# A decoder layer on one core: three waits in the first projection, the bias table and the last accumulators, and 256 columns of the last norm given to other engines

## The chip, the cores and the metric

The kernel runs on one core of a Trainium2 chip. A core has a matmul engine (TensorE, "PE" in the profile; its weight loads are listed apart as "PEld"), VectorE ("DVE"), ScalarE ("ACT"), GpSimd ("POOL") and SyncE ("SP", which only issues DMAs here). Each engine works through its own list of instructions in the order in which the program wrote it, and waits on semaphores for the others. The metric is the device time of one launch in microseconds (us).

## The reference

One decoder layer for x of 256 tokens by 2048 features, all in float32:

```
proj = x @ w_in                      # 2048 -> 18,768 columns: queries, shared latent, gates, indexer, RG-LRU input
attn = sparse attention: indexer scores, the best 64 keys of each query, softmax with a T5
       relative-position bias rel_bias[bucket(distance)], values projected up per head
h    = RG-LRU: causal depthwise convolution of width 4, gates, scan over the tokens
merged = sigmoid(g_A) * ((attn * silu(gate_a)) @ w_branch_a)
       + sigmoid(g_B) * ((h * silu(gate_b)) @ w_branch_b)
out  = layernorm(2**0.25 * x + merged @ w_out) * ln_g + ln_b
```

The three places of this change are the first part of the projection, the table of the relative-position bias, and the end: the product with w_out and the layer norm.

## The kernel before, in words

**Split operands.** Every float32 matrix is taken apart into a high part and a low part: `hi_of` (L97, ScalarE) copies it rounded to the type that TensorE takes, and `lo_of` (L101, VectorE) subtracts that copy from the original. A product is then the sum of three: high by high, high by low and low by high. So each weight tile costs a load (SP), a `hi` (ScalarE) and a `lo` (VectorE) before TensorE can use it.

**The first projection (L219 to L275).** The loop over k (16 steps of 128 features) multiplies all tokens by 848 columns (latent, indexer weights and key: psc; the first four query tiles of the indexer: psq). In step k the program writes, in this order: `split_a(k + 1)` for the next step, the loads, TensorE's products of step k, and from k = 12 on one call of `split_to`, which splits the first halves of the weight tiles of the main loop (`raw`, four buffers; `hi` and `lo`, five buffers each). All that stands on ScalarE and VectorE in the order in which it is written.

**The main loop.** The other columns and products are jobs, each of 4 or 16 ticks. In every tick TensorE gets its products, then `tick(t)` lets every helper whose time has come write its next step (a helper is a generator; `yield n` makes it sleep n ticks), and every second tick `split_to` and `load_to` write the split of the half that is five ahead and the load of the one that is nine ahead. TensorE uses one half in two ticks of a column job.

**The table.** `rel` (L424) is such a helper, started at tick 25. It issues the load of the one-hot buckets, writes the high part of the 32 x 16 bias values, sleeps, writes their low part on VectorE (L429), sleeps, and writes the two matmuls psrel (L434). ScalarE copies their result and GpSimd's DMAs lay it out for the attention heads.

**The end.** The product with w_out is made in four column groups of 512. For the first three (pso) both token blocks (t = 0 and 1, 128 tokens each) run together; `residual` adds alpha * x on VectorE (L828) and takes the statistics of the result with bn_stats (L829). For t = 0 it writes its result into `y` (SBUF), for t = 1 back into the accumulator (PSUM). The fourth group (psz) is made for t = 0 whole, and then for t = 1 in two halves of 256 columns; `normalise` for t = 0 is written between the two. `acc_tile` hands out four accumulator banks in turn.

`normalise` (L840) joins the statistics (L844), starts the square root (ScalarE L291, VectorE L292 to L299), and then treats the columns in pieces of 512. Three of four go through VectorE: `centre` (L851: subtract the mean, multiply by ln_g) and `finish` (L854: multiply by the root, add ln_b), followed by a store issued from SP (L855). The piece from column 1024 goes another way: ScalarE subtracts the mean (L860), GpSimd multiplies by ln_g (L861), ScalarE multiplies by the root (L868), GpSimd adds ln_b (L869), and ScalarE issues the store (L870).

Of the kernel before, what the change touches and what calls it, by code (L numbers as in the profile page):

```python
# [13 lines left out]
AF = mybir.ActivationFunctionType  # L14
# [4 lines left out]
P = 128  # L19
# [54 lines left out]
def layer(ctx, tc, ar, out):  # L74
    nc = tc.nc
# [20 lines left out]
    def hi_of(hi, src):  # L96
        nc.scalar.activation(hi, src, AF.Copy)  # L97

    def lo_of(lo, src, hi):

        nc.vector.tensor_sub(lo, src, f(hi))  # L101

    def acc_tile(name):
        return psum.tile([P, 512], F32, name=name, tag="acc", bufs=4)
# [4 lines left out]
    def slot(name, dt=F32R):  # L109
        return big.tile([P, 2 * T], dt, name=name, tag="slot", bufs=16)  # L110
# [68 lines left out]
    def split_to(n):  # L179
        while st["split"] < min(n, len(halves)):  # L180
            i = st["split"]
            load_to(i + 1)
            raw = raws.pop(i)
            if NO + 24 <= i < NO + 28:
                pieces = []
                for e in range(2):
                    hi, lo = slot(f"wh{i}_{e}"), slot(f"wl{i}_{e}")
                    c = raw[:, e * 512:(e + 1) * 512]
                    hi_of(hi, c)
                    lo_of(lo, c, hi)  # L190
                    pieces.append((hi, lo))
                parts[i] = pieces
            else:
                hi = wpool.tile([P, 1024], F32R, name=f"hi{i}", tag="hi", bufs=5)
                lo = wpool.tile([P, 1024], F32R, name=f"lo{i}", tag="lo", bufs=5)
                hi_of(hi, raw)
                lo_of(lo, raw, hi)
                parts[i] = (hi, lo)
            st["split"] += 1
# [21 lines left out]
    with pool("pha", side="right") as pha:  # L221
        ins = {}

        def load_a(k):
            xr = pha.tile([P, T], F32, name=f"xr{k}", tag="xr", bufs=4)
            nc.sync.dma_start(xr, ar["xT"][k])
            wr = pha.tile([P, NA], F32, name=f"wr{k}", tag="wr", bufs=4)
            if k == 0:
                nc.scalar.dma_start(wr[:, :A_Q], ar["wA"][k][:, :A_Q])
                nc.sync.dma_start(wr[:, A_Q:], ar["wA"][k][:, A_Q:])  # L230
            else:
                nc.sync.dma_start(wr, ar["wA"][k])
            ins[k] = (xr, wr)

        def split_a(k):
            xr, wr = ins.pop(k)
            hi_of(xs[:, k, :T], xr)
            lo_of(xs[:, k, T:], xr, xs[:, k, :T])
            hi = pha.tile([P, NA], F32R, name=f"ahi{k}", tag="ahi", bufs=3)
            lo = pha.tile([P, NA], F32R, name=f"alo{k}", tag="alo", bufs=3)  # L240
            for c in ([slice(0, A_Q), slice(A_Q, NA)] if k < 3 else [slice(0, NA)]):
                hi_of(hi[:, c], wr[:, c])
                lo_of(lo[:, c], wr[:, c], hi[:, c])
            return hi, lo

        for k in range(4):
            load_a(k)
        smalls = [(params, ar["params"]), (causal, ar["causal"]), (kvg, ar["kvg"].to_broadcast([P, DL])),
                  (relb, ar["relb"])]
        sp = {0: split_a(0)}  # L250
        for k in range(KT):
            if k + 1 < KT:
                sp[k + 1] = split_a(k + 1)
            if k + 4 < KT:
                load_a(k + 4)
            else:
                load_to(st["load"] + 1)
            if 8 <= k < 12:
                nc.sync.dma_start(*smalls[k - 8])
            hi, lo = sp.pop(k)  # L260
            fl = (k == 0, k == KT - 1)
            for t in range(2):
                o = psc[t][:, :A_Q]
                x_hi = xs[:, k, t * P:(t + 1) * P]
                x_lo = xs[:, k, T + t * P:T + (t + 1) * P]
                nc.tensor.matmul(o, x_hi, hi[:, :A_Q], start=fl[0], stop=False)
                nc.tensor.matmul(o, x_hi, lo[:, :A_Q], start=False, stop=False)
                nc.tensor.matmul(o, x_lo, hi[:, :A_Q], start=False, stop=fl[1])
            last = k == KT - 1
            for high in (False, True) if last else (True, False):  # L270
                for i in range(4):
                    w = (hi if high else lo)[:, A_Q + i * P:A_Q + (i + 1) * P]
                    mm(psq[i], w, xs[:, k, :], high, fl[0] and high, last and high)
            if k >= 12:
                split_to(k - 11)  # L275

    def evac(ps, name, dst=None):

# [145 lines left out]
    def rel():  # L424
        oh = idx.tile([32, VL], F32R, name="oh")
        nc.gpsimd.dma_start(oh, ar["onehot"])
        rb = idx.tile([32, 2, NH], F32R, name="rb")
        hi_of(rb[:, 0, :], relb)
        yield 6  # L429
        lo_of(rb[:, 1, :], relb, rb[:, 0, :])  # L430
        yield 2
        ps = aux_tile("psrel")
        for e in range(2):
            nc.tensor.matmul(ps[:NH, :], rb[:, e, :], oh, start=e == 0, stop=e == 1)  # L434
        yield
        v = idx.tile([NH, VL], F32, name="vrel")
        nc.scalar.activation(v, ps[:NH, :], AF.Copy, scale=DL ** 0.5)
        yield
        nc.gpsimd.dma_start(dv, v)
        for g in range(NH // HG):  # L440
            nc.gpsimd.dma_start(dz[g], bass.AP(tensor=dv.tensor, offset=dv.offset + g * SLAB,
                                               ap=[[0, P], [1, SLAB]]).rearrange("p (h v) -> p h v", h=HG))
            yield 10

    bias = {}
# [333 lines left out]
    for kind, i in jobs:  # L779
        rhs = us if kind in ("ba", "bb") else {k: xs[:, k, :] for k in range(KT)}  # L780
        chunk = kind in CHUNKS
        ps = [acc_tile(f"ps_{kind}{i}_{t}") for t in range(2)] if chunk else acc_tile(f"ps_{kind}{i}")
        for qt in range(ticks((kind, i))):
            t = at[kind, i] + qt
# [8 lines left out]
            if t == G0 + 14:  # L793
                rnn_stack.close()
                dec_stack = ExitStack()
                v = dec_stack.enter_context(pool("dec", side="right")).tile([P, 16, T], F32, name="decay")
            if t == FIN:
                dec_stack.close()
                fin = ctx.enter_context(pool("fin", side="right"))
                y = [fin.tile([P, DM], F32, name=f"y{e}") for e in range(2)]  # L800
                gb = [fin.tile([P, DM], F32, name=f"gb{e}") for e in range(2)]
# [4 lines left out]
            else:  # L806
                high = qt in (0, 3)
                w = parts[t // 2][0 if high else 1]
                for kk in range(8):
                    k = qt // 2 * 8 + kk  # L810
# [12 lines left out]
    tmp = [fin.tile([P, 4], F32, name=f"lt{t}") for t in range(2)]  # L823
# [14 lines left out]
    rows = []  # L838

    def normalise(t, ne):  # L840


        mean = mv[t][:, 0:1]
        nc.vector.bn_aggr(mv[t], st6[t][:, :ne, :])  # L844
        mine = [(c, v) for u, c, v in rows if u == t]
        (rest, v3), = [r for r in mine if r[0].start == 1024]
        mine.remove((rest, v3))
        yr = y[t][:, rest]

        def centre(c, v):  # L850
            nc.vector.scalar_tensor_tensor(v, v, mean, gb[0][:, c], op0=OP.subtract, op1=OP.mult)  # L851

        def finish(c, v):
            nc.vector.scalar_tensor_tensor(y[t][:, c], v, r, gb[1][:, c], op0=OP.mult, op1=OP.add)  # L854
            nc.sync.dma_start(out[t * P:(t + 1) * P, c], y[t][:, c])  # L855

        root = rsqrt(mv[t][:, 1:2], [tmp[t][:, i:i + 1] for i in range(3)], 1.0)
        next(root)
        nc.vector.tensor_scalar(tmp[t][:, 3:4], mean, -1.0, None, op0=OP.mult)
        nc.scalar.activation(yr, v3, AF.Identity, bias=tmp[t][:, 3:4])  # L860
        nc.gpsimd.tensor_mul(yr, yr, gb[0][:, rest])  # L861
        centre(*mine[0])
        next(root)
        try:
            next(root)
        except StopIteration as e:
            r = e.value
        nc.scalar.activation(yr, yr, AF.Identity, scale=r)  # L868
        nc.gpsimd.tensor_add(yr, yr, gb[1][:, rest])  # L869
        nc.scalar.dma_start(out[t * P:(t + 1) * P, rest], yr)  # L870
        finish(*mine[0])
        for m in mine[1:]:
            centre(*m)
            finish(*m)
# [16 lines left out]
    last = range(NO + 24, NO + 32)  # L891
    cuts = [[slice(0, 512)], [slice(0, 256), slice(256, 512)]]
    for t in range(2):
        ps = acc_tile(f"psz{t}")
        for e, c in enumerate(cuts[t]):
            for n in last:
                for i in range(2):
                    d = 2 * (n - NO - 24) + i
                    products(ps[:, c], parts[n], i, d, xs[:, d, :], t, c)
                tick(t0)  # L900
                t0 += 1
                split_to(len(halves))
            residual(t, slice(3 * 512 + c.start, 3 * 512 + c.stop), 3 + e, ps[:, c])
        rows[-len(cuts[t]):] = [(t, slice(3 * 512, 4 * 512), ps if t else y[t][:, 3 * 512:])]
        normalise(t, 3 + len(cuts[t]))
    assert not agenda, agenda

# [51 lines left out]
```

## Time and profile before

| what | us |
|---|---|
| median of 3 runs | 1035.03 (1034.36 to 1035.72) |
| profiled execution | 1034.45 |
| its span, first to last instruction | 1032.7 |
| TensorE busy | 1015.0 (98%) |
| VectorE busy | 678.8 (66%) |
| ScalarE busy | 551.6 (53%) |
| GpSimd busy | 82.0 (8%) |

The profile is one execution. A timeline lists an engine's instructions as start, duration, engine, line, operation, tile written and tiles read, their shapes, and in square brackets how long the engine stood idle before it and what ended that. A chain of waits goes back from the last instruction to whatever released each one. Times are us from the start of the span.

### The profile page before, as it was taken

How to read it: one execution, taken by the hardware profiler on the slowest of the kernel's cores; microseconds unless marked ns; L12 is line 12 of the kernel's file. 1: busy time of each engine (PE TensorE's matmuls, PEld its weight loads, DVE VectorE, ACT ScalarE, POOL GpSimd, SP SyncE). 2: the span in 40 equal slices, each digit the busy share in tenths (PEclk: the TensorE clock that was granted, in tenths of full speed). 3: DMA queues.
4: the chain of work that ended last, by engine and by line, in shares of the span. 5: the costliest groups of instructions: out<-in, count | busy, mean ns of one | idle time of the engine just before them, and what ended most of it. 6: DMA issues, size and time to landing. Idle time of an engine off the chain costs nothing.

```text
span 1032.7 us, 14867 instructions
## 1 busy us (share of the span) xinstructions
PE 1015.0 (98%) x5464; PEld 881.0 (85%) x5464; DVE 678.8 (66%) x1147; ACT 551.6 (53%) x910; POOL 82.0 (8%) x120
## 2 busy tenths in 40 slices
PE   9999999999999999999999999999999999999994
PEld 8888888998999988888888888888888888888884
DVE  6668775677677766544454888855577875566565
ACT  6666654555555565444334566588655554444431
POOL 0004312001111100000000000000500000000002
PEclk9999999999999999999999999999999999999997
DMA  9745877656566565665667666556666678666632
GB/s 306 265 144 171 276 252 233 194 171 178 170 189 174 183 184 162 185 191 196 192 196 213 196 186 194 171 183 190 193 190 185 200 252 283 186 192 190 186 120 82
DMA packets 61000, 201.41 MB, mean 195 GB/s; under 512 B 6608, under 2 KB 13136, under 8 KB 59904
## 3 DMA queue, kind: packets, MB, share of 16 engines
q1 hardware_dynamic: 59264, 191.29, 60.1%
q0 software_dynamic: 1232, 8.49, 2.1%
q8 instruction: 43, 0.70, 0.3%
q10 hardware_dynamic: 432, 0.70, 0.2%
q14 instruction: 29, 0.24, 0.1%
HBM read 198.31 MB, written 6.32 MB: 198 GB/s over the span
## 4 chain that ended last, share of the span: by engine, by line
PE 96%; DVE 2%; DMA 1%; issue 0%; ACT 0%; SPq 0%; DVEq 0%; ACTq 0%
PE ps_q L204 17%; PE ps_ag L204 9%; PE ps_rg L204 9%; PE ps_xr L204 9%; PE ps_ga L776 3%; PE ps_bb L776 3%; PE ps_gb L776 3%; PE ps_gb L775 3%; PE ps_ga L774 3%; PE ps_bb L774 3%; PE ps_ba L776 3%; PE ps_ba L774 3%; PE ps_bb L775 3%; PE ps_ga L775 3%; PE ps_gb L774 3%; PE ps_ba L775 3%
## 5 line engine op out<-in xcount | busy, mean ns | idle before, releaser
L101 DVE TENSOR_TENSOR lo<-raw,hi 128x1024 fp32r<-128x1024 f32 x324 | 399.5, 1234 | 307.1 <-ACT hi L97 303.3
L97 ACT ACTIVATE hi<-raw 128x1024 fp32r<-128x1024 f32 x324 | 341.5, 1054 | 175.6 <-PE ps_ba L776 52.6
L204 PE MATMUL ps_q<-xs,hi 128*128 128x512 f32 x512 | 122.4, 391 | 0.0
L204 PEld LDWEIGHTS ps_q<-xs,hi 128*128 128x128 f32 x512 | 94.0, 188 | 18.3
L204 PE MATMUL ps_q<-xs,lo 128*128 128x256 f32 x512 | 71.2, 283 | 0.0
L204 PEld LDWEIGHTS ps_q<-xs,lo 128*128 128x128 f32 x512 | 66.3, 190 | 1.4
L204 PE MATMUL ps_ag<-xs,hi 128*128 128x512 f32 x256 | 61.2, 391 | 0.0
L204 PE MATMUL ps_rg<-xs,hi 128*128 128x512 f32 x256 | 61.2, 391 | 0.0
L204 PE MATMUL ps_xr<-xs,hi 128*128 128x512 f32 x256 | 61.2, 391 | 0.0
L204 PEld LDWEIGHTS ps_rg<-xs,hi 128*128 128x128 f32 x256 | 47.1, 188 | 9.1
L204 PEld LDWEIGHTS ps_ag<-xs,hi 128*128 128x128 f32 x256 | 47.1, 188 | 9.1
L204 PEld LDWEIGHTS ps_xr<-xs,hi 128*128 128x128 f32 x256 | 47.0, 188 | 9.1
L774 PE MATMUL ps_bb<-hi,ub 128*128 128x512 f32 x128 | 50.4, 393 | 0.0
L774 PE MATMUL ps_ga<-hi,xs 128*128 128x512 f32 x128 | 50.0, 391 | 0.0
L776 PE MATMUL ps_bb<-hi,ub 128*128 128x512 f32 x128 | 49.9, 390 | 0.0
L776 PE MATMUL ps_ga<-hi,xs 128*128 128x512 f32 x128 | 49.9, 390 | 0.0
L776 PE MATMUL ps_gb<-hi,xs 128*128 128x512 f32 x128 | 49.9, 390 | 0.0
L775 PE MATMUL ps_gb<-lo,xs 128*128 128x512 f32 x128 | 49.8, 389 | 0.0
L775 PE MATMUL ps_ga<-lo,xs 128*128 128x512 f32 x128 | 49.8, 389 | 0.0
L775 PE MATMUL ps_bb<-lo,ub 128*128 128x512 f32 x128 | 49.8, 389 | 0.0
L774 PE MATMUL ps_ba<-hi,ua 128*128 128x512 f32 x128 | 49.8, 389 | 0.0
L775 PE MATMUL ps_ba<-lo,ua 128*128 128x512 f32 x128 | 49.8, 389 | 0.0
(273 smaller groups left out, 1888.7 us busy)
## 6 DMA issues: line engine op xcount, KB each, us to landing
raw<-in_wt SPq DMA_DIRECT2D x168, 512.0 KB, 4.2
raw<-in_wga SPq DMA_DIRECT2D x32, 512.0 KB, 3.6
raw<-in_wba SPq DMA_DIRECT2D x32, 512.0 KB, 3.5
raw<-in_wgb SPq DMA_DIRECT2D x32, 512.0 KB, 3.5
raw<-in_wbb SPq DMA_DIRECT2D x32, 512.0 KB, 3.7
raw<-in_wo SPq DMA_DIRECT2D x32, 512.0 KB, 3.6
wr<-in_wA SPq DMA_DIRECT2D x15, 424.0 KB, 4.6
dz<-dv POOLq DMA_DIRECT2D x4, 1024.0 KB, 8.6
```

The costliest lines, as they stand in the source:

```text
L97: nc.scalar.activation(hi, src, AF.Copy)
L101: nc.vector.tensor_sub(lo, src, f(hi))
L204: nc.tensor.matmul(ps[:, :n], w, rhs[:, :n], start=start, stop=stop)
L774: nc.tensor.matmul(o, mh, hi, start=d == 0, stop=False)
L775: nc.tensor.matmul(o, mh, lo, start=False, stop=False)
L776: nc.tensor.matmul(o, ml, hi, start=False, stop=d == KT - 1)
```

## The change

It makes four edits. The first call of `split_to` in the first projection comes one step later, so that three halves instead of four are split there and the main loop's first call splits two. The low part of the bias values is written 3 ticks after the high part instead of 6, and the matmul 5 ticks after that instead of 2. Each half of the last column group gets an accumulator tile of its own, and the norm treats the two halves of t = 1 as two pieces of 256. In `normalise`, columns 512 to 767 join those that ScalarE and GpSimd treat, after the piece from 1024, with a store of their own; columns 768 to 1023 stay with VectorE as a piece of 256.

```diff
--- before.py
+++ after.py
@@ -271,8 +271,8 @@
                 for i in range(4):
                     w = (hi if high else lo)[:, A_Q + i * P:A_Q + (i + 1) * P]
                     mm(psq[i], w, xs[:, k, :], high, fl[0] and high, last and high)
-            if k >= 12:
-                split_to(k - 11)
+            if k >= 13:
+                split_to(k - 12)
 
     def evac(ps, name, dst=None):
 
@@ -426,9 +426,9 @@
         nc.gpsimd.dma_start(oh, ar["onehot"])
         rb = idx.tile([32, 2, NH], F32R, name="rb")
         hi_of(rb[:, 0, :], relb)
-        yield 6
+        yield 3
         lo_of(rb[:, 1, :], relb, rb[:, 0, :])
-        yield 2
+        yield 5
         ps = aux_tile("psrel")
         for e in range(2):
             nc.tensor.matmul(ps[:NH, :], rb[:, e, :], oh, start=e == 0, stop=e == 1)
@@ -842,10 +842,14 @@
 
         mean = mv[t][:, 0:1]
         nc.vector.bn_aggr(mv[t], st6[t][:, :ne, :])
-        mine = [(c, v) for u, c, v in rows if u == t]
-        (rest, v3), = [r for r in mine if r[0].start == 1024]
-        mine.remove((rest, v3))
-        yr = y[t][:, rest]
+        mine, theirs = [], []
+        for c, v in [(c, v) for u, c, v in rows if u == t]:
+            if c.start == 512:
+                theirs.append((slice(512, 768), v[:, :256]))
+                mine.append((slice(768, 1024), v[:, 256:]))
+            else:
+                (theirs if c.start == 1024 else mine).append((c, v))
+        theirs.sort(key=lambda r: -r[0].start)
 
         def centre(c, v):
             nc.vector.scalar_tensor_tensor(v, v, mean, gb[0][:, c], op0=OP.subtract, op1=OP.mult)
@@ -857,17 +861,19 @@
         root = rsqrt(mv[t][:, 1:2], [tmp[t][:, i:i + 1] for i in range(3)], 1.0)
         next(root)
         nc.vector.tensor_scalar(tmp[t][:, 3:4], mean, -1.0, None, op0=OP.mult)
-        nc.scalar.activation(yr, v3, AF.Identity, bias=tmp[t][:, 3:4])
-        nc.gpsimd.tensor_mul(yr, yr, gb[0][:, rest])
+        for c, v in theirs:
+            nc.scalar.activation(y[t][:, c], v, AF.Identity, bias=tmp[t][:, 3:4])
+            nc.gpsimd.tensor_mul(y[t][:, c], y[t][:, c], gb[0][:, c])
         centre(*mine[0])
         next(root)
         try:
             next(root)
         except StopIteration as e:
             r = e.value
-        nc.scalar.activation(yr, yr, AF.Identity, scale=r)
-        nc.gpsimd.tensor_add(yr, yr, gb[1][:, rest])
-        nc.scalar.dma_start(out[t * P:(t + 1) * P, rest], yr)
+        for c, v in theirs:
+            nc.scalar.activation(y[t][:, c], y[t][:, c], AF.Identity, scale=r)
+            nc.gpsimd.tensor_add(y[t][:, c], y[t][:, c], gb[1][:, c])
+            nc.scalar.dma_start(out[t * P:(t + 1) * P, c], y[t][:, c])
         finish(*mine[0])
         for m in mine[1:]:
             centre(*m)
@@ -891,8 +897,8 @@
     last = range(NO + 24, NO + 32)
     cuts = [[slice(0, 512)], [slice(0, 256), slice(256, 512)]]
     for t in range(2):
-        ps = acc_tile(f"psz{t}")
         for e, c in enumerate(cuts[t]):
+            ps = acc_tile(f"psz{t}_{e}")
             for n in last:
                 for i in range(2):
                     d = 2 * (n - NO - 24) + i
@@ -901,7 +907,6 @@
                 t0 += 1
                 split_to(len(halves))
             residual(t, slice(3 * 512 + c.start, 3 * 512 + c.stop), 3 + e, ps[:, c])
-        rows[-len(cuts[t]):] = [(t, slice(3 * 512, 4 * 512), ps if t else y[t][:, 3 * 512:])]
         normalise(t, 3 + len(cuts[t]))
     assert not agenda, agenda
```

## Rows read from the trace of the kernel before

**Rows 1.** From the page: the chain that ended last, shares of the span by engine.
```profile
PE 96%; DVE 2%; DMA 1%; issue 0%; ACT 0%; SPq 0%; DVEq 0%; ACTq 0%
```
**Rows 2.** The waits of TensorE over the whole span: who waited for whom, us in total, times, longest.
```profile
PE psz L774 <- DVE st L829: 4.8, 1, 4.8
PE psrel L434 <- ACT hi L97: 1.3, 1, 1.3
...
PE psc L267 <- DVE alo L101: 0.4, 1, 0.4
```
**Rows 3.** TensorE's timeline at the end of the first projection: the first instruction of step k = 13, of k = 14, its second one, and the first of the main loop.
```profile
35.68 0.32 PE L266 MATMUL psc<-ahi,xs 128*128 128x336 f32 x1
...
38.01 0.32 PE L266 MATMUL psc<-ahi,xs 128*128 128x336 f32 x1
38.70 0.42 PE L267 MATMUL psc<-alo,xs 128*128 128x336 f32 x1 [0.37 <-DVE alo L101]
...
43.40 2.00 PE L204 MATMUL ps_qi<-xs,hi 128*128 128x512 f32 x8
```
**Rows 4.** The same stretch and the one behind it: two instructions of ScalarE's timeline, three of VectorE's and one of TensorE's.
```profile
35.04 1.06 ACT L97 ACTIVATE hi<-raw 128x1024 fp32r<-128x1024 f32 x1 [3.37 <-DMA raw<-in_wt]
...
36.31 0.90 ACT L97 ACTIVATE ahi<-wr 128x848 fp32r<-128x848 f32 x1
...
36.13 1.23 DVE L101 TENSOR_TENSOR lo<-raw,hi 128x1024 fp32r<-128x1024 f32 x1 [3.38 <-ACT hi L97]
...
37.61 1.03 DVE L101 TENSOR_TENSOR alo<-wr,ahi 128x848 fp32r<-128x848 f32 x1
...
46.18 0.42 DVE L284 TENSOR_TENSOR s_qi<-psq,r_qi 128x256 f32<-128x256 f32 x1
...
49.00 0.38 PE L333 MATMUL psk<-ident,kd 128*128 128x128 f32 x2
```
**Rows 5.** The table: two rows of TensorE's timeline, two of VectorE's, and the load of the one-hot buckets (KB, us from issue to landing).
```profile
95.04 0.40 PE L381 MATMUL pss<-ks,qis 128*128 128x256 f32 x2
96.73 0.63 PE L434 MATMUL psrel<-oh,rb 32*16 32x512 f32 x2 [1.29 <-ACT hi L97]
...
90.95 1.22 DVE L101 TENSOR_TENSOR lo<-raw,hi 128x1024 fp32r<-128x1024 f32 x1
...
96.27 0.16 DVE L101 TENSOR_TENSOR rb<-relb,rb 32x16 fp32r<-32x16 f32 x1
...
oh<-in_onehot POOLq DMA_DIRECT2D x1, 64.0 KB, 4.1
```
**Rows 6.** TensorE's timeline at the end: the last matmul of the first half of t = 1, the first of the second half, the 19th and the last of its 48; then two stretches with busy time of PE, PEld, DVE, ACT, POOL, the granted clock, the DMA share and GB/s.
```profile
1010.03 0.28 PE L776 MATMUL psz<-hi,xs 128*128 128x256 f32 x1
1015.16 0.39 PE L774 MATMUL psz<-wh,xs 128*128 128x256 f32 x1 [4.85 <-DVE st L829]
...
1018.90 0.29 PE L774 MATMUL psz<-wh,xs 128*128 128x256 f32 x1
...
1022.38 0.28 PE L776 MATMUL psz<-hi,xs 128*128 128x256 f32 x1
...
1004.00:1010.30 6.30, 6.30 (x51) 6.03 (x49) 4.70 (x10) 2.48 (x4) 1.29 (x1) 1.00 0.01 3
...
1015.20:1022.70 7.50, 7.46 (x48) 7.26 (x48) 0.00 (x1) 0.00 (x0) 0.00 (x0) 0.77 0.09 33
```
**Rows 7.** VectorE's timeline at the end: two of the three finishes of t = 0, the statistics of the first half of t = 1, the residual of its second half, and the first and last finish of t = 1.
```profile
1008.77 1.75 DVE L854 SCALAR_TENSOR_TENSOR y<-y,lt,gb 128x512 f32<-128x512 f32 x1
...
1011.22 1.63 DVE L854 SCALAR_TENSOR_TENSOR y<-y,lt,gb 128x512 f32<-128x512 f32 x1
...
1013.55 0.75 DVE L854 SCALAR_TENSOR_TENSOR y<-y,lt,gb 128x512 f32<-128x512 f32 x1
...
1014.67 0.43 DVE L829 BATCH_NORM_STATS2 st<-psz 128x6 f32<-128x256 f32 x1
1022.70 0.43 DVE L828 SCALAR_TENSOR_TENSOR psz<-y,psz 128x256 f32<-128x256 f32 x1 [7.59 <-PE psz L776]
...
1025.49 0.75 DVE L854 SCALAR_TENSOR_TENSOR y<-pso,lt,gb 128x512 f32<-128x512 f32 x1
...
1028.39 0.75 DVE L854 SCALAR_TENSOR_TENSOR y<-psz,lt,gb 128x512 f32<-128x512 f32 x1
```
**Rows 8.** The other engines at the end: GpSimd's first multiply of t = 0 and its add of t = 1, the last store issued from ScalarE and from SP; then groups of GpSimd and ScalarE on 256 columns over the whole span (busy us, mean ns of one | idle before), the stores (KB, us to landing), and one stretch with the GB/s last in it.
```profile
1008.69 1.29 POOL L861 TENSOR_TENSOR y<-y,gb 128x512 f32<-128x512 f32 x1 [164.75 <-ACT y L860]
...
1027.06 1.26 POOL L869 TENSOR_TENSOR y<-y,gb 128x512 f32<-128x512 f32 x1 [0.83 <-ACT y L868]
...
1028.36 0.34 ACTq L870 DMA_DIRECT2D out<-y  x1
...
1029.17 0.33 SPq L855 DMA_DIRECT2D out<-y  x1
...
L572 POOL TENSOR_TENSOR ag<-ag,s_ag 128x256 f32<-128x256 f32 x16 | 12.0, 750 | 48.9 <-ACT ag L570 48.8
...
L570 ACT ACTIVATE ag<-s_ag 128x256 f32<-128x256 f32 x16 | 6.7, 418 | 32.8 <-DVE s_ag L284 32.7
...
out<-y SPq DMA_DIRECT2D x6, 256.0 KB, 2.1
...
1029.20:1029.80 0.60, 0.00 (x0) 0.00 (x0) 0.00 (x0) 0.00 (x0) 0.00 (x0) 0.50 1.04 389
```

## The prediction

> **What bounds the kernel now.** I read the chain of waits first. TensorE holds 96% of it and everything else a few per cent [rows 1], so time can only go where TensorE stands still or runs slowly, or after its last matmul. The view of TensorE's waits, read next, names all of its idle time but the wait for the start: 4.8 us once before psz, 1.3 us once before psrel, 0.4 us once before psc [rows 2]. The three edits of this change go to these three places. For each I then read the timelines of the engines around it. The reader is to see in rows 3 to 5 which instruction came late and what stood ahead of it in its queue, and in rows 6 to 8 that after the largest wait TensorE also ran at a mean granted clock of 0.77 where it had 1.00 before (the lower level, 1.2 of 2.4 GHz, for part of the stretch), and that beyond its last matmul some 10 us of VectorE work and DMA follow.
>
> **First splits.** TensorE's steps k=13 and k=14 of the first projection start at 35.68 and 38.01, so a step takes 2.33. From the start of k=14 to the first ps_qi at 43.40 there are two steps, 5.39 where 4.66 would do: 0.73 is lost [rows 3]. The place is 38.70, where L267 waits for alo. That alo (37.61) stands on VectorE behind the lo of the first weight tile (36.13), its ahi (36.31) on ScalarE behind that tile's hi, and this hi waited until 35.04 for the transfer [rows 4]. The change puts the ahi of k=14 ahead of that hi. The next such pair, for k=15, then stands where the pair for k=14 stood, done by about 38.7, and TensorE asks for it only at 38.01 + 2.33 = 40.3. Term: -0.73.
> What is moved: no work goes; each of the first three splits goes out one step later, and the fourth goes into the first step of the main loop, ahead of the fifth. The transfers are issued as before, but the buffer of the fourth comes free later, by about two splits, for the load four halves on. That load has several halves of lead, and I cost it at nothing. VectorE gets 1.23 us more ahead of the first s_qi: 46.18 + 0.42 + 1.23 = 47.83, and the transposes psk that need its bank are at 49.00, or 48.27 after the gain [rows 4]. The cover is 0.4 us; if it is gone, the price is at most the 0.8 left of that split. Bounds: -0.73 to about 0.
>
> **Table.** psrel could start when the last pss pair has been issued, 95.04 + 2 x 0.12 = 95.28; it starts at 96.73. Its late operand is the lo of rb, a VectorE instruction of 0.16 us which runs only at 96.27, behind the lo of a weight tile. Emitted three ticks (one and a half splits) earlier, it stands near the lo of 90.95 [rows 5], four microseconds before it is needed. The two yields have the same sum, so psrel itself and all that follows keep their ticks. The onehot table, the other operand, is asked for eight ticks before psrel, over 11 us, and such a transfer lands in 4.1 [rows 5]. Term: -1.45; bound 0, if another operand were as late.
> Both gains shift all later work alike. TensorE has no other wait until psz [rows 2], so nothing there is already waiting on a slower engine.
>
> **Last accumulators.** The last matmul of token block 1's first half starts at 1010.03, and the first one of its second half at 1015.16. It waits for the bn_stats of the first half, which ends at 1014.67 + 0.43 = 1015.10 [rows 7]: both halves lie in one tile, and that reading stands on VectorE behind the whole norm of block 0. Then 18 steps take until 1018.90 (0.208 each), and the last 29 until 1022.38 (0.12 each) [rows 6]. With a tile for each half TensorE runs on at 0.12: 1010.03 + 48 x 0.12 = 1015.79 in place of 1022.38, so -6.59, of which 18 x 0.088 = 1.58 is clock and 5.01 standing. The new tile's bank was last that of an accumulator whose residual is long done, four allocations back.
> What is late next: VectorE must have finished block 0's norm and the first residual by 1016.07. That list ends at 1015.10 now. It loses one 512-column pair (1.45, half of the two pairs from 1025.49 to 1028.39) and gains a 256-column pair (2 x 0.43), so -0.59. Against that stands the Pool engine: 0.75 when nothing runs beside it, but 1.75 beside a Pool multiply [rows 7], which started 0.08 earlier and took 1.29 [rows 8]. Pool gets two more operations of 0.75. Fully serial, from 1008.69: Pool 1.29 + 0.75 + 1.26 + 0.75 = 4.05, VectorE 0.75 + 0.86 + 1.45 + 0.88 = 3.94, end 1016.68. At best it is 1014.51. I take 1015.3, nearer to the row of before, with its lost time scaled by Pool's work: hidden by 0.8 us.
> The Trainium skill (SBUF — State Buffer, "Who interferes with whom") says that VectorE reading two inputs from SBUF and a GpSimd operation reading SBUF block each other fully, by order of issue. By that rule the serial end, 1016.68, is the sum, and block 1 starts 0.6 late. The trace bears it out for operands in SBUF (1.75 against 0.75).
>
> **Last norm.** For block 1 VectorE's operands come from PSUM, and its 0.75 at 1025.49 beside a Pool operation shows no loss. Its pairs become 512, 256, 256, 256: two pairs of 512 after the first (2.90) become three of 256 (at most 3 x 0.86), so it ends 0.3 to 0.45 earlier than 1028.39 + 0.75 [rows 7]. But it is no longer last. ScalarE's queue holds, in order: scale 512, the DMA issue of these columns, which waits for Pool's add, then scale 256. Queued behind that waiting issue are the scale and, through it, Pool's last add and the last DMA. In times of before: add ends 1027.06 + 1.26 = 1028.32; issue 1028.36 + 0.34; scale 0.42 [rows 8] to 1029.14; Pool 0.1 + 0.75; issue at 1030.03, where the last issue was at 1029.17: +0.86. The transfer is half of 256 KB, at 389 GB/s 0.34 shorter [rows 8]: +0.52. No row shows 256-column stores, so the bounds are -0.4 (the issue holds nothing up and VectorE ends it) and +0.86 (they land in the same 2.1). I take +0.55.
> That ScalarE's compute stands behind the waiting issue is no row of before; the Trainium skill (PSUM — Partial Sum Buffer, "Engine vs sequencer instructions") calls the queue strictly first in, first out. By it the term is positive, without it negative.
>
> **Sum.** -0.73 - 1.45 - 6.59 + 0.55 = -8.22. The profiled execution took 1034.45 (span 1032.7 and 1.75 around it), so 1026.2 for it; the median of the runs shown is 0.58 above it: 1026.8.
>
> **Rivals.**
> *The port decides:* Pool and VectorE go one after the other in block 0, and the statistics of block 1 wait for VectorE, not TensorE. For: 1.75 and 1.63 beside Pool, 0.75 without. Against: half of Pool's work finds VectorE waiting for something else. 0.6 to 0.9 of the gain goes: 1027.6.
> *The front is hidden anyway:* another operand of psc and psrel is nearly as late. For: ScalarE's splits run close there. Against: no second wait in the rows. 2.2 less: 1029.0.
> *The tail is not lengthened:* the scale isn't held up, 0.55 + 0.4 more: 1025.8.
> *The accumulators don't part:* TensorE still waits at psz, since the new tile's bank or the semaphore still hangs on VectorE's list. For: the wait names bn_stats, which that list holds up. Against: the rotation of four. Only the front gains, minus the tail: 1035.03 - 2.18 + 0.55 = 1033.4, and up to 1034.9 with the serial list.
> *Slower:* that same wait becomes longer. Place: psz, second half. The serial list ends at 1016.68 instead of 1015.10, +1.6, and the longer standing leaves all 48 steps at the lower level: another 30 x 0.088 = 2.6. With the tail 0.55 against the front's 2.18: +2.6, 1037.6. It decides against the change once stall and clock together cost over 1.6 more than now. Against it: the banks part in the diff.
>
> **How the numbers follow.** Forecast 0.64, port 0.15, front hidden 0.08, shorter tail 0.08, no parting 0.03, slower 0.02. The runs before spread from 1034.36 to 1035.72, so the forecast alone spans 1026.0 to 1027.6. With the port, the shorter tail, and half of the hidden front the range is 1025.5 to 1028.7. Under 0.2% (2.1 us) a difference counts as none here: faster 0.95 (the first four), same 0.03, slower 0.02.
>
> **What would show it.** Right: no TensorE wait in the changed kernel beyond the start; first ps_qi at 42.7; psrel directly behind pss near 94.5; psz steps of 0.12 throughout at full clock; the last DMA issue on ScalarE's queue, about 0.9 after where VectorE's would have been. Wrong: a wait of psz for bn_stats; a residual of block 1's second half that starts more than 0.1 after the last matmul (the port); the last issue on SP. A saving under 6 us or over 10 would contradict the sum.

## The result

The changed kernel takes 1030.41 us (median of 7 runs, 1028.64 to 1032.44) against 1035.03 of the one before (1034.15 to 1037.73 in 7 runs): a ratio of 0.9949, 95% interval 0.9934 to 0.9965. It is faster, by 4.6 us, where 8.2 were forecast; the time lies above the predicted range. The profiled execution took 1030.43 with a span of 1028.2, against 1034.45 and 1032.7: the span lost 4.5, the time around it went from 1.75 to 2.2.

### The profile after

The waits of TensorE over the whole span in the changed kernel: of the three of [rows 2], those before psz and psc are gone, and the one before psrel has grown.

```profile
PE psrel L434 <- ACT hi L97: 2.0, 1, 2.0
PE warm L217 <- DVE eps L139: 1.0, 1, 1.0
```

TensorE's timeline of the changed kernel at the places of [rows 3] and [rows 5], and behind psrel:

```profile
42.72 2.01 PE L204 MATMUL ps_qi<-xs,hi 128*128 128x512 f32 x8
...
94.38 0.40 PE L381 MATMUL pss<-ks,qis 128*128 128x256 f32 x2
96.73 0.63 PE L434 MATMUL psrel<-oh,rb 32*16 32x512 f32 x2 [1.95 <-ACT hi L97]
97.29 1.68 PE L204 MATMUL ps_ag<-xs,lo 128*128 128x256 f32 x8
98.77 4.99 PE L204 MATMUL ps_ag<-xs,hi 128*128 128x512 f32 x16
```

The first projection ends 0.68 earlier, as worked out. But psrel starts at 96.73, to the hundredth where it did before, and TensorE has only stood longer. VectorE's timeline of the changed kernel shows what stands ahead of that start:

```profile
90.95 0.15 DVE L101 TENSOR_TENSOR rb<-relb,rb 32x16 fp32r<-32x16 f32 x1
...
95.20 1.23 DVE L101 TENSOR_TENSOR lo<-raw,hi 128x1024 fp32r<-128x1024 f32 x1 [0.78 <-ACT hi L97]
96.34 0.48 DVE L390 TENSOR_TENSOR rl<-pss,rl 128x128 f32<-128x128 f32 x2
```

The low part of the table runs at 90.95, as meant, 5.8 us before psrel. What ends just ahead of psrel is the first of the two instructions of L390 (0.28 each): 96.34 + 0.28 = 96.62. It is the last reader of the first of the two pss tiles of the fifth score. `aux_tile` hands out four banks in turn, two tiles per score, so psrel gets the bank of that very tile. The row stood in the trace of before too, directly behind the rb row at 96.27 that I quoted in [rows 5]:

```profile
96.36 0.47 DVE L390 TENSOR_TENSOR rl<-pss,rl 128x128 f32<-128x128 f32 x2
```

The chain of waits of the changed kernel gives a hint of it. Its columns are start, us and what; the third piece has no cause and lasts 0.34, where psz in [rows 6] followed its releaser after 0.06 (1015.10 and 1015.16):

```profile
95.07 0.36 ACT r_ag L280
95.43 0.95 ACT hi L97
96.39 0.34 issue
96.73 0.63 PE psrel L434 x2
```

Behind the longer standing the clock fell. The stretches of the changed kernel after psrel (busy time of PE, PEld, DVE, ACT, POOL, granted clock, DMA share, GB/s) go down to half, the lower level of 1.2 GHz, and back:

```profile
97.00:98.00 1.00, 1.00 (x7) 0.71 (x6) 0.95 (x1) 0.85 (x2) 1.00 (x1) 0.90 0.51 66
98.00:99.00 1.00, 1.00 (x6) 1.00 (x6) 0.63 (x2) 0.00 (x0) 1.00 (x3) 0.50 0.92 344
...
101.00:102.00 1.00, 1.00 (x6) 0.81 (x5) 1.00 (x1) 0.05 (x1) 0.00 (x0) 0.89 0.70 283
102.00:103.00 1.00, 1.00 (x6) 0.83 (x5) 0.52 (x3) 1.00 (x2) 0.00 (x0) 1.00 0.15 43
```

In the kernel before it had stayed at 1.00 through all of these stretches; one of them:

```profile
98.00:99.00 1.00, 1.00 (x8) 0.91 (x7) 0.62 (x2) 0.00 (x0) 1.00 (x3) 1.00 0.93 311
```

From here on TensorE is 1.59 later than before, until the last accumulators. These lines answer to [rows 6] to [rows 8]: TensorE's timeline (the last matmul of the first half of t = 1, the first and the last of the second half), VectorE's and ScalarE's.

```profile
1011.63 0.28 PE L776 MATMUL psz<-hi,xs 128*128 128x256 f32 x1
1011.75 0.28 PE L774 MATMUL psz<-wh,xs 128*128 128x256 f32 x1
...
1017.39 0.28 PE L776 MATMUL psz<-hi,xs 128*128 128x256 f32 x1
```
```profile
1010.37 1.75 DVE L858 SCALAR_TENSOR_TENSOR y<-y,lt,gb 128x512 f32<-128x512 f32 x1
1012.04 0.96 DVE L855 SCALAR_TENSOR_TENSOR y<-y,mv,gb 128x256 f32<-128x256 f32 x1
1013.04 1.41 DVE L858 SCALAR_TENSOR_TENSOR y<-y,lt,gb 128x256 f32<-128x256 f32 x1
...
1016.83 0.43 DVE L829 BATCH_NORM_STATS2 st<-psz 128x6 f32<-128x256 f32 x1
1017.70 0.43 DVE L828 SCALAR_TENSOR_TENSOR psz<-y,psz 128x256 f32<-128x256 f32 x1 [0.44 <-PE psz L776]
...
1023.52 0.48 DVE L858 SCALAR_TENSOR_TENSOR y<-psz,lt,gb 128x256 f32<-128x256 f32 x1
```
```profile
1023.37 0.34 ACTq L876 DMA_DIRECT2D out<-y  x1
1023.75 0.51 ACT L874 ACTIVATE y<-y,lt 128x256 f32<-128x256 f32 x1 [1.76 <-POOL y L875]
1025.09 0.34 ACTq L876 DMA_DIRECT2D out<-y  x1
```

The two halves follow each other at 0.12 with no wait. VectorE is through with block 0 and the first half's statistics at 1017.26, 0.4 before the last matmul ends, so block 1 starts on TensorE's time. The last store is ScalarE's, 7.42 after the end of the last matmul; before it was SP's, 6.51 after it.

So the sum for the spans of these two profiles is: first splits -0.68, given back as +0.68 of longer standing at psrel, whose own start didn't move (0); the clock behind it +1.59; the accumulators -6.59; the norm +0.49. Together -4.51, and 4.5 were measured.

### The profile page after: what moved, and what is told of

Same layout as the page of the kernel before. It is cut to its first block, busy times and chain, and to the rows that moved or that the text cites. A ratio compares the mean times of both kernels' runs of the same rounds, so it can differ in the third digit from the quotient of the medians.

```text
span 1028.2 us, 14883 instructions
## 1 busy us (share of the span) xinstructions
PE 1014.6 (99%) x5464; PEld 880.8 (86%) x5464; DVE 680.3 (66%) x1149; ACT 553.9 (54%) x914; POOL 85.7 (8%) x124
## 4 chain that ended last, share of the span: by engine, by line
PE 98%; DMA 0%; DVE 0%; ACT 0%; issue 0%; POOL 0%; SPq 0%; POOLq 0%; ACTq 0%
PE ps_q L204 17%; PE ps_ag L204 9%; PE ps_rg L204 9%; PE ps_xr L204 9%; PE ps_bb L776 3%; PE ps_ga L774 3%; PE ps_ga L776 3%; PE ps_gb L775 3%; PE ps_bb L774 3%; PE ps_gb L776 3%; PE ps_ba L776 3%; PE ps_ga L775 3%; PE ps_bb L775 3%; PE ps_ba L774 3%; PE ps_ba L775 3%; PE ps_gb L774 3%
```

## The experiments

The theory, called "bank" in the expectations: psrel waits for a bank that VectorE frees at its own pace, so that nothing in front of it can gain, and standing longer there can cost clock. Its rivals: the edits simply add up and were each worth less; the one-hot transfer lands late; ScalarE, whom the profile names, holds psrel up; the low part was late after all. Ratios are to the kernel before.

| kernel | median us | ratio, 95% interval | span of the profile |
|---|---|---|---|
| changed | 1030.41 | 0.9949 (0.9934 to 0.9965) | 1028.2 |
| accumulators alone | 1028.42 | 0.9939 (0.9927 to 0.9952) | 1026.6 |
| changed, first splits undone | 1028.95 | 0.9944 (0.9932 to 0.9957) | 1026.6 |
| changed, psrel on another ring | 1026.99 | 0.9923 (0.9911 to 0.9936) | 1024.9 |
| the same, table edit undone | 1029.56 | 0.9948 (0.9934 to 0.9961) | 1026.3 |
| changed, psrel two ticks later | 1028.23 | 0.9928 (0.9916 to 0.9940) | 1026.3 |
| changed, table edit undone | 1030.02 | 0.9943 (0.9931 to 0.9955) | 1030.0 |
| changed, psrel's wait filled | 1029.18 | 0.9939 (0.9927 to 0.9952) | 1026.6 |
| changed, once more | 1029.17 | 0.9947 (0.9933 to 0.9960) | 1026.7 |
| psrel on another ring, norm undone | 1026.15 | 0.9908 (0.9895 to 0.9921) | 1024.2 |
| psrel on another ring, stores last | 1026.48 | 0.9913 (0.9900 to 0.9926) | 1024.1 |

**Accumulators alone**, in the kernel before:

```diff
     for t in range(2):
-        ps = acc_tile(f"psz{t}")
         for e, c in enumerate(cuts[t]):
+            ps = acc_tile(f"psz{t}_{e}")
...
-        rows[-len(cuts[t]):] = [(t, slice(3 * 512, 4 * 512), ps if t else y[t][:, 3 * 512:])]
```

> The kernel before with the last accumulators parted alone (first splits, table and norm as before). Theory 'bank': the front edits of the change gave nothing, since psrel starts at 96.73 in both kernels whatever arrives earlier, and the longer standing there cost 1.6 us of clock; so this edit alone should keep psrel's idle time at 1.3 us, the granted clock at 1.00 behind it, and save the 6.6 us of the psz wait: about 1028.4, that is 0.9936 of before, and faster than the whole change by 1.5 to 2.5 us. Rival 'the sum': the four edits add up, and this one alone gives no more than the whole change, 1030.4 or above. The statistics of token block 1 start within 0.1 us of the last matmul.

1028.42, as the bank theory said. In this profile the standing at psrel is 1.3, and the clock behind it stays at 1.00. The last matmul starts at 1016.26 instead of 1022.38, which is 6.12 less, although this execution reached the first ps_qi 0.48 later than the one of before (43.88 for 43.40): together 6.60. One edit of the four gives as much as all of them together, or more. How much more is not shown: the difference to the changed kernel's median is of the size expected (2.0), but the two intervals overlap, and against the median of all its 12 runs (below), 1029.79, it is 1.4.

**First splits undone:**

```diff
-            if k >= 13:
-                split_to(k - 12)
+            if k >= 12:
+                split_to(k - 11)
```

> The changed kernel with the edit of the first splits undone. Theory 'bank': TensorE comes to psrel 0.7 us later, psrel still starts at about 96.7, its idle time falls from 1.95 to about 1.3 us, the granted clock stays at 1.00 between 97 and 103 and the span is 1.6 us shorter than that of the changed kernel (about 1026.6), although an edit that by itself shortens the first projection was taken out. Rival 'the splits are worth their 0.7': the span is 0.7 longer, 1028.9, and psrel starts later.

Again as the theory said. TensorE is back at 43.40 for the first ps_qi, and its timeline shows psrel where it was, after a shorter wait:

```profile
95.02 0.40 PE L381 MATMUL pss<-ks,qis 128*128 128x256 f32 x2
96.72 0.63 PE L434 MATMUL psrel<-oh,rb 32*16 32x512 f32 x2 [1.30 <-ACT hi L97]
```

The clock stayed at 1.00, and the span is 1.6 shorter, although 0.7 of work in front was given back. An edit that does what it should was worth nothing here, since the next wait swallows it. That it does harm is not shown: another execution of the changed kernel ("once more", below) also kept its clock, and its span of 1026.7 is the same as here.

**psrel on another ring**, that of the accumulators:

```diff
-        ps = aux_tile("psrel")
+        ps = acc_tile("psrel")
```

> The changed kernel with psrel's accumulator taken from the other ring of four banks, so that it doesn't wait for the bank that a score tile held. Theory 'bank': no TensorE wait at psrel, which starts at about 94.6 behind the pss pair, granted clock 1.00 throughout, span shorter than the changed kernel's by 0.68 + 1.45 + 1.59 = 3.7, about 1024.5, time about 1026.7. Rival 'one-hot': the transfer of the one-hot buckets lands late; psrel still starts at 96.7 and nothing changes. Rival 'ScalarE', whom the profile names: psrel waits for a hi of a weight tile; nothing changes either.

This settles it: one word, and 3.4 us between the medians (2.8 against the median of all 12 runs of the changed kernel; 1.8 of span against its execution that kept its clock). TensorE's and VectorE's timelines of this kernel:

```profile
94.73 0.40 PE L381 MATMUL pss<-ks,qis 128*128 128x256 f32 x2
95.06 0.63 PE L434 MATMUL psrel<-oh,rb 32*16 32x512 f32 x2
```
```profile
96.71 0.48 DVE L390 TENSOR_TENSOR rl<-pss,rl 128x128 f32<-128x128 f32 x2
```

psrel follows the scores without a wait, while L390 is as late as ever: TensorE simply no longer needs it. The transfer and ScalarE's work were left as they were, so both rivals fall. The single runs lie between 1026.71 and 1027.14, where those of the changed kernel spread over 3.8 us.

**The same with the table edit undone:**

```diff
-        yield 3
+        yield 6
         lo_of(rb[:, 1, :], relb, rb[:, 0, :])
-        yield 5
+        yield 2
```

> As the run with psrel's own bank, but with the table edit undone (low part six ticks after the high part, matmul two ticks later). Theory 'bank': now the low part is the late operand; it runs near 96.3 on VectorE, psrel waits for it until about 96.5 and starts 0.2 earlier than in the changed kernel at most, with the clock loss as there: about 1030.2 against 1026.7 with the edit. So the edit is worth about 3.5 us with a free bank, and nothing without. If the low part was never late, this run equals the one with the edit.

Now the low part is late, and only now. TensorE issues the first matmul of psrel, with the high part, and waits before the second for the low one; here the profile names the true releaser:

```profile
94.92 0.40 PE L434 MATMUL psrel<-oh,rb 32*16 32x512 f32 x1
96.69 0.40 PE L434 MATMUL psrel<-oh,rb 32*16 32x512 f32 x1 [1.37 <-DVE rb L101]
```
```profile
96.48 0.16 DVE L101 TENSOR_TENSOR rb<-relb,rb 32x16 fp32r<-32x16 f32 x1
```

It costs 2.6 us in the medians (3.5 expected) and 1.4 in the spans of the two profiles; in this profile the clock stayed at 1.00. The runs at 1029.56 and above have a mean clock of 0.994 or 0.995, this one 0.996, so there it may have fallen; they have no profile. So the table edit is right, but behind a second wait of the same length.

**Table edit alone undone**, psrel on its old ring (the same diff as above, in the changed kernel):

```diff
-        yield 3
+        yield 6
...
-        yield 5
+        yield 2
```

> The changed kernel with the table edit alone undone. Theory 'bank': the low part runs near 96.3 and is done before the score tile is read (96.6), so psrel starts at 96.7 as in the changed kernel, after 1.95 us of standing, with the clock loss behind it: same as the changed kernel, 1030.4 (within 1). Rival 'low part': the edit was worth its 1.45 us, and without it the time is 1031.9 and psrel starts later.

1030.02, the same as the changed kernel within its spread: without a free bank the edit is worth nothing. The profiled execution was the slowest of six. psrel waits 1.94, and two stretches behind it show the clock down for longer than in the changed kernel's profile:

```profile
97.06 1.01 PE L434 MATMUL psrel<-oh,rb 32*16 32x512 f32 x2 [1.94 <-ACT hi L97]
```
```profile
98.00:100.00 2.00, 2.00 (x10) 2.00 (x10) 1.58 (x6) 0.75 (x2) 1.70 (x3) 0.50 0.93 256
...
102.00:104.00 2.00, 2.00 (x6) 1.59 (x5) 0.86 (x3) 0.48 (x2) 0.90 (x2) 0.53 0.39 83
```

**psrel two ticks later**, on its old ring:

```diff
         lo_of(rb[:, 1, :], relb, rb[:, 0, :])
-        yield 5
+        yield 7
```

> The changed kernel with psrel written two ticks later, still on the ring of the score tiles. Theory 'bank': psrel's bank is free by then and it doesn't wait, but it still takes a turn of the ring, so TensorE meets the same lateness of VectorE two ticks on: pss of the seventh score waits 1 to 1.5 us for the bank that the sixth score's first tile held (read by VectorE near 102.2). Less than the 1.95 of the changed kernel, so no clock loss: about 1028.0 to 1028.5. Rival 'only psrel was late': no wait at all, 1027.0.

The wait moved to where the ring said, the second tile of the seventh score, and ends with the same line of VectorE, one score later:

```profile
101.54 0.40 PE L381 MATMUL pss<-ks,qis 128*128 128x256 f32 x2
102.93 0.36 PE L379 MATMUL pss<-ks,qis 128*128 128x256 f32 x1 [0.99 <-DVE rl L390]
```
```profile
102.50 0.48 DVE L390 TENSOR_TENSOR rl<-pss,rl 128x128 f32<-128x128 f32 x2
```

The median, 1028.23, lies in the range expected and above the 1027.0 of the rival.

**psrel's wait filled** with work that nobody reads, and **the changed kernel once more** beside it:

```diff
+        fill = acc_tile("fill")
+        for i in range(28):
+            nc.tensor.matmul(fill[:, :P], zero, zero, start=True, stop=True)
         ps = aux_tile("psrel")
```

> The changed kernel with 28 small matmuls of zeros (128 x 128, into a bank of the other ring, result unused) written ahead of psrel, so that TensorE works through most of the wait. Theory 'standing costs clock': psrel still starts near 96.7, since its bank isn't freed earlier, but the granted clock stays at 1.00 behind it and the 1.6 us come back: span about 1026.6 and every run near 1028.8, without the spread of the changed kernel (1028.6 to 1032.4). Rival 'the clock falls for another reason' (psrel's small shape, say): it falls again, 1030.4.

> The changed kernel itself, for the same chip as the filled one: 1030.4, single runs anywhere from 1028.6 to 1032.4 with mean clocks from 0.997 down to 0.993, by how long the clock stays down behind psrel.

TensorE's timeline of the filled kernel, and a stretch behind psrel:

```profile
94.56 1.74 PE L434 MATMUL fill<-zero 128*128 128x128 bf16 x28
96.67 0.63 PE L437 MATMUL psrel<-oh,rb 32*16 32x512 f32 x2 [0.38 <-ACT hi L97]
```
```profile
98.00:100.00 2.00, 2.00 (x12) 1.70 (x11) 1.69 (x5) 0.55 (x2) 1.31 (x3) 1.00 0.99 277
```

psrel starts where it did, the clock stays up, and the five runs lie between 1028.69 and 1029.44. But my expectation for the changed kernel was too firm. In its profile here TensorE stood just as long and kept its clock:

```profile
96.81 0.63 PE L434 MATMUL psrel<-oh,rb 32*16 32x512 f32 x2 [1.96 <-ACT hi L97]
```
```profile
98.00:100.00 2.00, 2.00 (x12) 1.74 (x12) 1.58 (x6) 0.47 (x3) 1.45 (x3) 1.00 0.86 268
```

Its five runs go from 1028.74 to 1030.95 and their median, 1029.17, equals that of the filled kernel. So a standing of some 1.95 us brings the clock down in some executions and not in others. Of the changed kernel's 12 runs in all, 6 lie at 1029.2 or below and 6 at 1030.4 or above; the profile of one of the lower kept its clock, that of one of the upper lost it. That the filled kernel avoids it fits (no run of five above 1029.44), but it is not shown by the medians of this pair.

**Norm undone**, with psrel on the other ring:

```diff
-            if c.start == 512:
-                theirs.append((slice(512, 768), v[:, :256]))
-                mine.append((slice(768, 1024), v[:, 256:]))
-            else:
-                (theirs if c.start == 1024 else mine).append((c, v))
+            (theirs if c.start == 1024 else mine).append((c, v))
```

> psrel on its own bank, and the edit of the last norm undone (columns 512 to 1023 whole on VectorE, as before). Theory 'queue': in the changed kernel the last store is issued on ScalarE's queue 7.4 us after the last matmul, because the scale of the 256 columns stands behind the issue that waits for Pool's 512-column add; without the edit VectorE's last finish is the end, 6.9 us after the last matmul. So the edit of the norm costs 0.5 us and undoing it gives 1026.5 against 1027.0. Rival 'less for VectorE': the norm's end follows VectorE's work, which the edit shortens by a 256-column pair; undoing it costs 0.3 to 0.5, 1027.4.

The best median of all, 0.84 less than with the norm's edit. The two ran on different chips, and the intervals of their ratios overlap; no single run of one reaches those of the other. TensorE's last matmul and VectorE's last finish:

```profile
1013.82 0.28 PE L776 MATMUL psz<-hi,xs 128*128 128x256 f32 x1
```
```profile
1020.49 0.48 DVE L854 SCALAR_TENSOR_TENSOR y<-psz,lt,gb 128x256 f32<-128x256 f32 x1
```

From 1014.10 to 1020.97 are 6.9, as expected. The span is 0.7 shorter than with the norm's edit (1024.2 and 1024.9), but 0.3 of that has nothing to do with the norm. TensorE's last matmul comes 0.29 later in the other kernel's profile, where TensorE had waited near the start for a hi part whose weights had landed late:

```profile
7.71 0.42 PE L266 MATMUL psc<-ahi,xs 128*128 128x336 f32 x1 [0.21 <-ACT ahi L97]
...
1014.11 0.28 PE L776 MATMUL psz<-hi,xs 128*128 128x256 f32 x1
```

From the end of the last matmul to the end of the span are 10.1 here and 10.5 there: that 0.4 is the norm's. The time around the span is back at 1.76 (1025.96 against 1024.2 in the profiled run), which is another 0.45.

**Stores last**, with psrel on the other ring and the norm as changed:

```diff
             nc.gpsimd.tensor_add(y[t][:, c], y[t][:, c], gb[1][:, c])
+        for c, v in theirs:
             nc.scalar.dma_start(out[t * P:(t + 1) * P, c], y[t][:, c])
```

> psrel on its own bank, the norm as changed, but with both stores of ScalarE's queue issued after both scales. Theory 'queue': the 256-column scale runs as soon as the 512-column one is done, Pool's two adds follow each other, and the last issue comes about 6.4 us after the last matmul instead of 7.4, level with VectorE's: 1.0 less, 1026.0, and the best of all. Rival 'Pool is the limit': Pool's four operations set the end by themselves and nothing changes, 1027.0.

Half right. The last matmul of this kernel ends at 1014.04, and ScalarE's queue:

```profile
1017.64 1.20 ACT L874 ACTIVATE y<-y,lt 128x512 f32<-128x512 f32 x2 [1.01 <-DVE y L858]
1019.74 1.04 ACTq L877 DMA_DIRECT2D out<-y  x2
```

The 256-column scale follows the 512-column one directly, and the last issue, 1019.74 + 1.04 - 0.34 = 1020.44, comes 6.4 after the last matmul instead of 7.4. But only some 0.4 of the 1.0 reach the end of the span: it lies 10.1 behind the last matmul, where it was 10.5 (the spans differ by 0.8, the other 0.35 lie ahead of the last matmul, as above). The medians differ by 0.5. The stores now lie closer together, and the moving of bytes (343 to 371 GB/s between 1020.7 and 1021.9) ends some 1.8 after the last issue, where it was 1.3 with the issues apart (near 1022.2 and 1023.1). It doesn't beat undoing the edit.

## Why the prediction was wrong

**The step that failed is "Table"**: "Its late operand is the lo of rb". It was one of two things that ended about 0.2 us apart on the same engine (96.43 and 96.64), and the later one was not an operand but the bank. I checked the inputs of psrel (high part, low part, one-hot) and not where its output goes, though for psz I had counted the ring of four. The term of -1.45 measured 0. With a free bank the whole front is worth 3.3 of span (the run on the other ring against the changed kernel, 1.6 of it clock). The table edit alone is worth 1.4 of span there; the first splits alone were not tried with a free bank.

**The second error hangs on it**: "Both gains shift all later work alike. TensorE has no other wait until psz". The view of waits can show only what is late now; whoever arrives earlier finds the waits that were covered. The -0.73 of the first splits measured -0.68 at 42.72 and was gone at 96.73. VectorE's L390 ran at 96.36 before and 96.34 after, whatever TensorE had gained.

**Not forecast at all**: the standing grew from 1.29 to 1.95 and the clock fell, +1.59 in the profiled execution (the same standing left it up in another, so this part is not forced). I had read the fall behind the 4.85 at psz [rows 6], and never asked what a longer wait at psrel would do.

**The rival "the front is hidden anyway"** had this as its mechanism ("another operand ... is nearly as late") and 1029.0 as its time; with the clock's loss it would have been 1030.6. It got 0.08. The argument against it, no second wait in the rows, was the error: a wait has one row, whatever number of things it waits for. The prediction's own signs say the same: psrel at 96.73 instead of near 94.5, a wait left there, and a saving of 4.6, under the 6 us below which it had said the sum would be contradicted.

**Right were**: the accumulators, -6.59 forecast and measured, of which the run of this edit alone shows the whole (6.60 at the last matmul). The list of VectorE in block 0 ended, less the 1.59, at 1015.67 for my 1015.3: hidden, with 0.4 of cover instead of 0.8. The rule of the Trainium skill (SBUF — State Buffer, "Who interferes with whom") shows in the rows, 1.41 for a 256-column finish of block 0 where block 1's, with one input in PSUM, takes 0.48, but not as a fully serial sum, which would have ended at 1016.68. The scale behind the waiting issue stands in the rows as written: the issue at 1023.37, the scale at 1023.75, the last issue at 1025.09; with the issues written last, the scale follows the other directly. So the trace agrees with the Trainium skill (PSUM — Partial Sum Buffer, "Engine vs sequencer instructions") that the queue is first in, first out. The span's term was +0.49 for my +0.55; a 256-column finish took 0.48 where I had 0.43.

**Mis-sized**: the norm costs about 0.9 in time, 0.4 to 0.5 of span and 0.45 around it (0.84 between the two medians). The sum took those 1.75 us around the span as fixed.

With psrel off the ring, where the steps hold as I had them, the kernel takes 1026.99 for my 1026.8. That it comes so close is partly luck: its profiled execution took 1027.14 where the sum gives 1026.2 for one, 0.4 more in the span and 0.45 around it, and the 0.58 that I added for the median did not appear.

## What to carry to other kernels

Before a wait is costed as removable, list everything that the waiting instruction needs, its output bank too, with its last reader; a piece without a cause between the named releaser and the start says that somebody else released it. A gain far ahead of the end counts only up to the next place where engines meet, and there it can turn into longer standing. Run the edits apart: one that is hidden behind another's wait looks worthless and can be right. And before a difference of a few tenths is put down to an edit near the end, look whether it already stands ahead of that place.

## What was not expected of the hardware

The same kernel, standing 1.95 and 1.96 us at the same place, ran on at a granted clock of 0.50 for over three microseconds in one execution and at 1.00 in another; after 0.99, 1.30 and 1.37 us it stayed at 1.00 in every profile here. In the kernel without the table edit it was down from about 97 to 104 after 1.94. What decides between them is open.

The time around the span was 1.75 to 1.8 us in kernels with one store per token block on ScalarE's queue, and 2.2 in all those with two. Two of them, on the other ring with and without the norm's edit, differ by that edit alone; why it costs 0.45 there was not tried.
